# An eight-tap causal convolution on TensorE: another order of its head, dummy matmuls before the first product, and one mid weight summed by DMA

## The chip, the cores and the metric

The kernel runs on one core of a Trainium2 chip. The metric is device time in microseconds (us), as a median over several executions. A trace covers one execution and gives a span that is, in the runs of this case, 1.74 to 2.2 us shorter than the time reported for the same execution.

Engines are named as in the profile: PE is TensorE, DVE is VectorE, ACT is ScalarE, POOL is GpSimd, SP is SyncE. PEld is PE's weight load.

## The reference

```python
# x: (8, 4096, 512) float32, kernel: (8, 512, 512) float32
out = np.zeros_like(x)
for k in range(8):
    shifted = x if k == 0 else np.concatenate(
        [np.zeros((B, k, D), np.float32), x[:, :-k, :]], axis=1)
    out += np.matmul(shifted, kernel[k])
```

Every output row is a sum of eight rows of x, each multiplied by its own 512x512 matrix ("tap").

## The kernel before

The kernel cuts the 32,768 rows into 128 runs of 256 consecutive rows. One run lies on each SBUF partition, and a step handles eight rows of every run, so there are 32 steps. Each step needs x transposed. In steady state an SP DMA does that (`transpose_x`). The first rows are transposed by PE itself: its 16 transposes at 24.51 us took 1.07 us, where a transposed load takes 6.1 us (median).

It saves products by working with sums of x rows (`D4`, `D42`, `D421` and so on, made by DVE) and differences of weights (the "mid" weights, `W[MID, ...]`). A "product" is four matmuls of 128x128 by 128x512: one row of every run by one 512x512 matrix. A step has three "nodes", each for four rows and four taps. A node makes nine products instead of 16 (36 matmuls) and combines them in PSUM through "seeds": copies that ACT writes into a PSUM bank, onto which PE then accumulates. The very first node is computed directly, with 16 products.

The parts that the change and the argument touch:

```python
    def load_x(i, h):                                  # POOL, 512 KB into SBUF
        xin[i, h] = xpool.tile([P, 4, D], bf, name="xin")
        load(xin[i, h], xr[:, K * i + 4 * h:K * i + 4 * h + 4, :])

    def transpose_x(i, h):                             # SP, SBUF to SBUF, transposing
        nc.sync.dma_start_transpose(out=XT[:, 4*h:4*h+4, :]..., in_=xin[i, h]...)

    def mid_dve(*which):                               # DVE, 128x2048 subtraction
        o, u, v = mid(*which)
        tt(o, u, v, SUB)

    def fill(pw):                                      # a pair of dummy matmuls
        for h in range(2):
            nc.tensor.matmul(pw[:, h], lhsT=zero[:, 0:P], rhs=zero, start=True, stop=True)

    def node_seed(n, b_):                              # ACT writes the seed into PSUM
        n.p[b_] = pair((2 * n.k + b_) % 3)
        if b_ == LO: nc.scalar.copy(out=n.p[b_][:, 1], in_=n.q[:, 1])
        else:        nc.scalar.mul(out=n.p[b_][:, 1], in_=n.q[:, 1], mul=-1.0)
    # ... cut ...
    # the head, in program order (cut to what matters)
    transpose_pe("h0", 3, H, 4, 6)                     # rows before the run (history)
    transpose_pe("h1", 0, H, 6, 8)
    nc.scalar.copy(out=to(XF[:, 0:2]), in_=prev(bank["h0"]))
    transpose_pe("x0", 2, xin[0, 0], 0, 2)             # first x rows
    nc.scalar.copy(out=XF[:, 4:6], in_=bank["x0"])
    tt(D4[:, 0:2], XF[:, 0:2], XF[:, 4:6], ADD)
    transpose_pe("xb", 3, xin[0, 0], 2, 4)
    direct(0, 0)                                       # first product: first tap
    # ... cut: nine more products, DVE sums and mid weights ...
    transpose_pe("x1", 2, xin[0, 1], 0, 4)
    # ... cut ...
    transpose_pe("x2", 2, xin[1, 0], 0, 4)             # second step's first x rows, all four
    tt(T4, XT[:, 4:8], XT[:, 0:4], ADD)
    direct(3, 0); fill(pair(2)); direct(3, 1)
    node_a1(1)                                         # needs a DVE sum, then an ACT copy
    # ... cut ...
    mid_dve(0, HI, LO)                                 # the mid weight that the change moves
    # ... cut; then the loop over nodes, the same in both kernels:
    for k, (i, a) in enumerate(order):
        if a == MID and more: transpose_x(i + 1, 0)
        # ... products, seeds, sums ...
        if a == LO and more:
            transpose_x(i + 1, 1)
            load_x(i + 2, 0); load_x(i + 2, 1)
```

## Time and profile before

| | before |
|---|---|
| time, median of 3 | 780.17 us (780.01 to 780.49) |
| traced span | 778.4 us |
| transposed loads (SP), median | 6.1 us from issue to landing, 61 of them |

How busy each engine is, as a whole and stage by stage, and where PE stops is read in the prediction below. Two views that matter later were not used for the prediction. One is the list of DMA queues, from which this line comes; it gives packets, megabytes and the share of the 16 DMA engines.

```profile
q8 instruction: 28, 0.46, 0.2%
```

The reader is to see 28 transfers of about 16 KB each in a queue of their own. 0.2% looks like nothing.

The other is the timeline well inside the steady part. Here are DVE and ACT of the kernel before, around 103 us (start, busy time, engine, line, operation, count; in brackets the idle time before and who ended it):

```profile
102.78 1.23 DVE L76 TENSOR_TENSOR D<-XT 128x2048 bf16<-128x2048 bf16 x1 [0.37 <-DMA XT<-xin]
103.93 1.22 DVE L76 TENSOR_TENSOR y<-pp,ms 128x1024 f32<-128x1024 f32 x1
...
105.98 0.57 ACT L249 COPY pp<-pp 128x512 f32<-128x512 f32 x1 [0.71 <-PE pp L190]
```

DVE waits 0.37 us for a transposed load, then makes the sum D4 and, behind it, the output y, done at 105.15. ACT's seed at 105.98 waits for PE, not for y. With the 0.08 us that a handover from y to the seed takes (seen in the trace after: y done 106.02, seed 106.10), this load could land 0.75 us later before PE felt it.

### The profile page before, as it was taken

The page shows a single profiled execution, that of the slowest core. Times are in us where ns is not written, and L with a number is a line of the kernel's source. Part 1 is how long each engine was busy: PE and PEld are TensorE (multiplying, and loading weights), DVE is VectorE, ACT ScalarE, POOL GpSimd, SP SyncE. Part 2 cuts the span into 40 slices and gives each one's busy share as a digit, 9 for nine tenths or more (in the row PEclk, how much of TensorE's full clock was granted, in tenths as well). Part 3 has the DMA queues.
Part 4 walks back from the last instruction along what each step waited for, and adds up shares of the span by engine and source line. Part 5 has one row for each costly group of instructions (what it writes and reads, how often), then busy time and mean ns, then how long its engine had stood idle before and what let it go on. Part 6 is the DMA issues. An engine that isn't in the chain of part 4 may idle for free.

```text
span 778.4 us, 9432 instructions
## 1 busy us (share of the span) xinstructions
PE 765.6 (98%) x3576; PEld 346.9 (45%) x3576; DVE 658.7 (85%) x767; ACT 282.7 (36%) x461; POOL 41.2 (5%) x79
## 2 busy tenths in 40 slices
PE   6999999999999999999999999999999999999997
PEld 3444444444444444444444444444444444444443
DVE  4999988898888898888898888898888898878895
ACT  3453343333343333343333343333343333343332
POOL 4000000000000000000000000000000000000000
PEclk9999999999999999999999999999999999999999
DMA  9975887877787878787787687877797867687843
GB/s 198 211 125 137 214 198 181 194 166 185 166 177 194 195 166 177 171 194 179 175 189 183 166 202 170 195 168 185 166 192 176 204 162 185 167 181 184 205 132 122
DMA packets 159229, 138.90 MB, mean 178 GB/s; under 512 B 130128, under 2 KB 134224, under 8 KB 159056
## 3 DMA queue, kind: packets, MB, share of 16 engines
q1 hardware_dynamic: 145456, 99.89, 46.0%
q0 software_dynamic: 13584, 38.15, 31.1%
q8 instruction: 28, 0.46, 0.2%
q10 hardware_dynamic: 144, 0.26, 0.1%
q14 instruction: 17, 0.14, 0.1%
HBM read 77.33 MB, written 67.11 MB: 186 GB/s over the span
## 4 chain that ended last, share of the span: by engine, by line
PE 92%; DVE 4%; DMA 2%; issue 1%; POOL 1%; DVEq 0%; ACT 0%; ACTq 0%; POOLq 0%
PE pp L190 92%; DMA xin<-in_x_dram 2%; DVE w L76 2%; DVE D L76 1%; POOL w L80 0%; DVE pp L76 0%; DVE pp L265 0%; DVE XT L383 0%; PE pp L179 0%; DVE y L76 0%; DVE A L76 0%; POOL xin L80 0%; DVEq L635 0%; ACT pp L249 0%; POOL XT L80 0%
## 5 line engine op out<-in xcount | busy, mean ns | idle before, releaser
L190 PE MATMUL pp<-w,D 128*128 128x512 bf16 x3280 | 716.8, 379 | 4.2 <-DMA w<-in_kernel_dram 2.6
L190 PEld LDWEIGHTS <-D 128*128 128x128 bf16 x3280 | 320.4, 98 | 392.8 <-issue 3.3
L76 DVE TENSOR_TENSOR D<-D 128x1024 bf16<-128x1024 bf16 (+1 forms) x252 | 228.4, 945 | 1.0 <-ACT D L346 0.9
L76 DVE TENSOR_TENSOR y<-pp,ms 128x1024 f32<-128x1024 f32 (+1 forms) x121 | 146.2, 1211 | 45.4 <-PE pp L190 45.4
L76 DVE TENSOR_TENSOR D<-XT 128x2048 bf16<-128x2048 bf16 (+2 forms) x153 | 142.3, 945 | 11.2 <-DMA XT<-xin 9.2
L237 ACT COPY pp<-pp 128x512 f32<-128x512 f32 x95 | 54.1, 570 | 255.1 <-PE pp L190 255.0
L249 ACT COPY pp<-pp 128x512 f32<-128x512 f32 x95 | 54.2, 570 | 172.2 <-PE pp L190 170.0
L76 DVE TENSOR_TENSOR pp<-dts,pp 128x512 f32<-128x512 f32 x95 | 65.5, 689 | 43.9 <-ACT dts L255 42.6
L292 ACT COPY ms<-pp 128x1024 f32<-128x1024 f32 x60 | 61.0, 1016 | 33.0 <-PE pp L190 33.0
L80 POOL DMA_DIRECT2D xin<-in_x_dram x64 | 34.0, 532 | 687.2 <-DMA XT<-xin 672.6
L265 DVE SCALAR_TENSOR_TENSOR pp<-pp,dts 128x512 f32<-128x512 f32 x95 | 65.8, 693 | 3.3
L255 ACT COPY dts<-pp 128x512 f32<-128x512 f32 x95 | 57.5, 606 | 2.0 <-PE pp L190 2.0
L251 ACT ACTIVATE pp<-pp 128x512 f32<-128x512 f32 x95 | 56.1, 590 | 0.8 <-DVE y L76 0.8
L190 PE MATMUL pp<-w,XT 128*128 128x512 bf16 x120 | 30.8, 379 | 0.0
L76 DVE TENSOR_TENSOR w<-w,w 128x2048 bf16<-128x2048 bf16 x19 | 22.8, 1217 | 0.3 <-DMA w<-in_kernel_dram 0.2
L190 PEld LDWEIGHTS <-XT 128*128 128x128 bf16 x120 | 11.7, 98 | 14.2
L190 PE MATMUL pp<-w,w 128*128 128x512 bf16 x36 | 9.2, 378 | 1.3 <-ACT pp L237 0.7
L190 PE MATMUL pp<-w,F 128*128 128x512 bf16 x36 | 8.9, 379 | 0.0
L391 ACT COPY XT<-pp 128x1024 bf16<-128x1024 bf16 x1 | 1.0, 1012 | 17.5 <-PE pp L179 17.5
L173 PE MATMUL pp<-zero 128*128 128x512 bf16 x16 | 6.1, 539 | 1.2 <-DVE zero L145 1.2
L331 DVE MEMSET D<- 128x64 bf16 x2 | 0.2, 112 | 7.9 <-ACT D L343 7.7
L80 POOL DMA_DIRECT2D w<-in_kernel_dram x8 | 6.0, 755 | 4.1 <-DMA w<-in_kernel_dram 3.0
(53 smaller groups left out, 69.9 us busy)
## 6 DMA issues: line engine op xcount, KB each, us to landing
out_dram<-y SPq DMA_DIRECT2D x123, 512.0 KB, 3.5
xin<-in_x_dram POOLq DMA_DIRECT2D x64, 512.0 KB, 5.8
w<-in_kernel_dram POOLq DMA_DIRECT2D x8, 512.0 KB, 17.5
D<-in_x_dram SPq DMA_DIRECT2D x1, 1024.0 KB, 4.9
out_dram<-ms SPq DMA_DIRECT2D x2, 512.0 KB, 3.2
out_dram<-f SPq DMA_DIRECT2D x2, 512.0 KB, 4.3
XT<-xin SPq DMA_TRANSPOSE x61, 6.1
XT<-in_x_dram POOLq DMA_DIRECT2D x1, 384.0 KB, 10.9
```

The source lines that it names most:

```text
L76: nc.vector.tensor_tensor(out=o, in0=a, in1=b, op=op)
L80: nc.gpsimd.dma_start(out=out, in_=src)
L173: nc.tensor.matmul(pw[:, h], lhsT=zero[:, 0:P], rhs=zero, start=True, stop=True)
L190: nc.tensor.matmul(bank, lhsT=comp[:, c * P:(c + 1) * P], rhs=w[:, c, :], start=start and c == 0, stop=c == DC - 1, skip_group_check=True)
L237: nc.scalar.copy(out=n.q[:, 0], in_=n.q[:, 1])
L249: nc.scalar.copy(out=n.p[b_][:, 1], in_=n.q[:, 1])
L251: nc.scalar.mul(out=n.p[b_][:, 1], in_=n.q[:, 1], mul=-1.0)
L255: nc.scalar.copy(out=n.dts, in_=n.q[:, 0])
L265: nc.vector.scalar_tensor_tensor(out=p[:, 0], in0=p[:, 1], scalar=-1.0, in1=n.dts, op0=MUL, op1=SUB)
L292: nc.scalar.copy(out=ms[b_], in_=p)
L331: nc.vector.memset(z[:, :, 0:D:G], 0.0)
L391: nc.scalar.copy(out=XT[:, 0:2], in_=bank["x2"][:, 0:2])
```

## The change

Its intent is to bring PE's steady stream forward by three means.

1. Three more pairs of dummy matmuls before the first product, to keep PE busy while it waits; the order of copies and transposes is changed with them. In the trace of before, PE's granted clock was 0.50 from 11.48 to 14.89 us, behind a stretch of 3.42 us with PE busy 1.16; that more work in the waiting time would keep it at 1.00 was the estimate from that.
2. The second step's first four x rows are loaded, transposed and summed two by two, so that the first node can start before all four are there.
3. The mid weight `W[MID, HI, LO]` is no longer a DVE subtraction. ACT writes the negated weight, and a GpSimd-issued DMA adds the other weight to it.

The remaining lines of the diff reorder the first seven nodes around this. The loop is untouched.

```diff
+    def mid_neg(u, v):
+        nc.scalar.mul(out=W[MID, u, v], in_=W[LO, u, v], mul=-1.0)
+    def mid_acc(u, v):
+        nc.gpsimd.dma_start(out=W[MID, u, v], in_=W[HI, u, v], accum_op=ADD)
 ... cut ...
+    fill(pair(2))
     transpose_pe("h0", 3, H, 4, 6)
+    nc.scalar.copy(out=to(XF[:, 0:2]), in_=prev(bank["h0"]))
+    fill(pair(2))
     transpose_pe("h1", 0, H, 6, 8)
-    transpose_pe("x0", 2, xin[0, 0], 0, 2)
+    transpose_pe("x0", 1, xin[0, 0], 0, 2)
 ... cut ...
-    transpose_pe("xb", 3, xin[0, 0], 2, 4)
+    transpose_pe("xb", 0, xin[0, 0], 2, 4)
+    fill(pair(2))
     direct(0, 0)
 ... cut ...
-    load_x(1, 0)
+    load_x(1, 0, 0, 2)
+    load_x(1, 0, 2, 4)
+    mid_neg(HI, LO)
 ... cut ...
-    transpose_pe("x2", 2, xin[1, 0], 0, 4)
+    transpose_pe("x2", 3, xin[1, 0], 0, 2)
+    transpose_pe("x3", 2, xin[1, 0], 2, 4)
+    fill(pair(3))
-    tt(T4, XT[:, 4:8], XT[:, 0:4], ADD)
+    tt(T4[:, 0:2], XT[:, 4:6], XT[:, 0:2], ADD)
+    tt(D41[:, 1], T4[:, 0], T4[:, 1], ADD)
+    node_a1(1)
+    direct(3, 0)
+    tt(T4[:, 2:4], XT[:, 6:8], XT[:, 2:4], ADD)
+    fill(pair(2))
 ... cut ...
+    mid_acc(HI, LO)
-    mid_dve(0, HI, LO)
```

## The prediction

> **What bounds the kernel now.** I read the page's busy shares first, then the stretches by stage, then TensorE's timeline and the chain that ended last for the first 61 us.
>
> ```profile
> PE 765.6 (98%) x3576; PEld 346.9 (45%) x3576; DVE 658.7 (85%) x767; ACT 282.7 (36%) x461; POOL 41.2 (5%) x79
> ```
>
> TensorE (PE) is busy 98% of the 778.4 us span. That is an average, so I cut the run into stages; in each row come the stretch, its length, the busy us and instruction count of PE, PEld, DVE, ACT and POOL, then the granted TensorE clock.
>
> ```profile
> 4.65:8.06 3.41, 1.98 (x20) 1.08 (x19) 0.00 (x0) 2.41 (x3) 1.87 (x3) 1.00 1.05 199
> 8.06:11.48 3.42, 1.16 (x21) 0.98 (x18) 1.54 (x5) 2.41 (x3) 1.29 (x2) 1.00 1.17 193
> 11.48:14.89 3.41, 3.11 (x12) 1.47 (x13) 2.06 (x2) 0.00 (x0) 1.49 (x2) 0.50 1.11 188
> 14.89:24.51 9.62, 8.46 (x45) 3.83 (x43) 8.75 (x10) 0.00 (x0) 0.74 (x1) 1.00 1.18 210
> 24.51:60.67 36.16, 34.38 (x178) 15.78 (x179) 35.25 (x43) 21.69 (x30) 2.14 (x4) 1.00 0.89 151
> 60.67:773.92 713.25, 713.09 (x3300) 322.56 (x3300) 609.48 (x707) 254.91 (x426) 30.12 (x57) 1.00 0.76 179
> ```
>
> From 60.67 us on PE has 3300 instructions in 713.25 us, 0.216 us each, and its gaps come to 0.16 us. The change leaves the loop and this arithmetic alone. So all that can be won lies before 60.67 us, and the end moves by as much as PE's stream is early at that point. In 24.51 to 60.67 DVE is busy 35.25 of 36.16 us: there the vector engine is nearly full too.
>
> ```profile
> 11.78 1.87 PE L190 MATMUL pp<-w,D 128*128 128x512 bf16 x4 [2.56 <-DMA w<-in_kernel_dram]
> 13.44 1.06 PE L173 MATMUL pp<-zero 128*128 128x512 bf16 x2
> 14.29 1.12 PE L179 MATMUL pp<-ident,XT 128*128 128x128 bf16 x12
> 16.47 4.48 PE L190 MATMUL pp<-w,D 128*128 128x512 bf16 x20 [1.05 <-DVE w L76]
> ...
> 24.51 1.07 PE L179 MATMUL pp<-ident,xin 128*128 128x128 bf16 x16
> ...
> 33.63 1.02 PE L190 MATMUL pp<-w,w 128*128 128x512 bf16 x4 [0.66 <-ACT pp L237]
> ...
> 36.18 2.02 PE L190 MATMUL pp<-w,w 128*128 128x512 bf16 x8 [0.66 <-ACT pp L249]
> ...
> 52.63 6.27 PE L190 MATMUL pp<-w,D 128*128 128x512 bf16 x28 [0.35 <-ACT pp L251]
> ```
>
> Start, busy time, engine, line, tiles, count, and in brackets the idle time and who ended it. The first tap ends a 2.56 us wait at 11.78. Its four matmuls start 0.42 us apart, because the clock is at 0.50 then. The chain that ended last (start, length, what) gives the next gate:
>
> ```profile
> 5.94 18.53 DMA xin<-in_x_dram
> 24.51 1.08 PE pp L179 x16
> 25.61 1.24 DVE XT L383
> ```
>
> The second half of the first x rows is issued at 5.94 and lands at 5.94 + 18.53 = 24.47; its transposes start at 24.51. After that this chain runs through DVE up to 60.67.
>
> [...] the clock changes at 11.48 and 14.89, 3.41 us apart, and the half-speed window follows one in which PE was busy only 1.16 of 3.42 us. One busy 1.98 of 3.41 was followed by full clock[...]. [...] queued loads here land about 2.5 us apart (24.47, then 26.56, 29.10, 31.64)[...]. [...] The before trace has none, so its duration is my largest unknown.
>
> **Part 1, the dummy matmuls and the order up to 24.5 us.** Added ahead of the first tap are three pairs of dummy matmuls. At full speed 6 x 0.216 = 1.3 us, all in waiting time. If they keep the clock up, the four first-tap matmuls and the following dummies and transposes save (1.87 + 1.06 + 1.12) / 2, about 2.0 us of engine time at most. But I expect almost nothing of it at the end. First, the transposes of x rows 2-3 now write the bank that held h1, and wait for ScalarE's third copy. ScalarE: copy of h0 from about 8.4, of x0 from 9.8, of h1 from 10.7, at 1.0 us each, so those transposes move from 8.6 to about 11.7. The window 8.06 to 11.48 then has h1, x0 and one dummy pair, some 1.4 us busy of 3.4[...]. The clock may drop all the same.
>
> Second, what follows is gated twice. DVE: copy of xb 12.4, D2 13.1 (1.4 us), D4 14.4, E4 15.1 to 16.0; the products that reuse E4's bank start at 16.1, against 16.47 before. From there PE has 9 products of 4 matmuls plus one dummy pair: 38 x 0.216 = 8.2 us, giving 24.3. In both kernels the same ten products stand ahead of the x1 transposes, which need the load that lands at 24.47. That load's place in the queue is unchanged. So x1 starts at 24.5 in both (24.7 with a dropped clock): **gain 0, perhaps -0.2**.
>
> **Part 2, x rows two by two, from 24.5 us.** The split halves land about 25.7 and 27.0; PE needs them at 27.1 and 27.6: no wait. Before, from 24.51: 16 transposes (0.90), two products (0.86 each), 16 transposes, three products, one dummy pair (0.43), a product, then the first A1 product at 31.94, a 0.82 us stop for ScalarE's copy, next product at 33.63. After: the same work with one dummy pair more, and A1 brought forward ahead of the last direct product, so that this product and the dummy pair cover the copy: A1 at 31.1, the last direct 31.9 to 32.8, dummies to 33.2, next product 33.2. DVE must have D41 ready for A1: copy 25.6, D4 26.9, D41 28.1, D42 28.7, T4 (half, 0.69 instead of 1.23) 29.9, D41 30.5 to 30.9. It fits by 0.2 us. Gain **0.4 us** (33.63 - 33.2): the stop of 0.82 less the dummy pair of 0.43. The stop for the seed at 36.18 stays, since nothing is put between.
>
> **Part 3, one mid weight by ScalarE and DMA.** DVE loses one 128x2048 subtraction: 1.22 us, 1.14 in steps from start to start. ScalarE gains a scaled copy of 128x2048, estimated 1.9 us from its copy of that size in this trace (1.91), in time it idles (17.5 us of idle before its first copy of x2). One sum of 0.42 us also moves before the x1 copy, and splitting T4 costs 0.15. So DVE is ahead by some 1.4 us at 60 us, and less on the way. PE's losses between 36.2 and 60.7, from start-to-start times: 0.13 at 37.2, 0.22 at 46.06, 0.51 at 52.63, 0.05 and 0.21 later; together 1.1 us. The one at 46.06 waits for a DVE subtraction behind D4, which needs the transposed x landing at 43.74, and will hold PE to 0.2 to 0.4 of lead there. The one at 52.63 waits for a ScalarE seed that the new order makes first: gone. The last two follow from DVE's mid weights, which come 0.6 to 1.4 us sooner: mostly gone.
>
> **Sum.** 0 + lead of 0.2 to 0.4 at 46 + 0.5 + 0.2 = **about 1.0 us** earlier, 0.13% of 780.17: 779.2.
>
> **Rivals.** (a) The DMA add lands late. It is issued behind the load that before started at 44.26 and took 6.7 us beside transposes; so issue near 45.5. [...] I estimate 6 to 9 us, landing at 51.5 to 54.5. DVE wants it at about 54.9 (55.47 before). A landing at 57 would stop DVE, then PE, and make 780 to 782. I give a stop 30%. For it: that load's 6.7 us. Against: the DMA engines are partly idle around 45 and 53. (b) The warm clock is worth its whole 2 us because the x1 load lands sooner: 777.5. Against it, the DMA share is over 1.0 in every stretch from 4.65 to 24.51, with the same loads in the same order; 5%. (c) The new order opens stops, such as A1 waiting for DVE with 0.2 us of margin, or later x loads delaying transposes: 779.5 to 781; 20%. (d) Everything at 24.5 to 60.7 is hidden behind DVE and nothing moves: 780.0; 20%.
>
> **Range and chances.** Runs of before spread 0.5 us. My 80% range is 777.9 to 780.8. Faster by 2% means 764.6; even all stops after 24.51 are under 3 us, so it is out of reach but for an error of mine. Slower by 2% needs 15.6 us, which only a gross stall of the DMA add would make.
>
> **What the profile after will show.** Right: x1 transposes at 24.5 with a longer PE wait before them or a start of 16.1 for the second products; A1 about 31.1 and no 0.82 us stop behind it; PE's steady stream reached about 1.0 us sooner; DVE with one fewer subtraction; the DMA add landed before its reader. Wrong: x1 at 23 or sooner, a DVE wait on the DMA add, or a PE wait for T4 or D41 at 31 us.

The forecast's sum came to about 1.0 us (0 for part 1, a lead of 0.2 to 0.4 at 46 us, 0.5 and 0.2), so 779.2 us. "The before trace has none" means a DMA that adds. The 6 to 9 us for it are the estimate; beside them is the 6.7 us of the load ahead of it.

## The result, and the profile after

The changed kernel took 780.79 us (780.42 to 781.59, 4 runs) against 780.09 us (779.83 to 780.49, 4 runs) for the kernel before on the same chip: 1.001, with a 95% interval of 0.9993 to 1.0027. A ratio here is the mean time of one kernel's fast runs over the mean of the other's in the same rounds, so it is not quite the ratio of the two medians. The prediction was 779.2 us: about 1.0 us to win, and none was won.

Line numbers move by nine from before to after: products are L199 (L190 before), transposes L188 (L179), dummies L182 (L173), the first seed L258 (L249). First the busy shares of the changed kernel:

```profile
PE 767.3 (99%) x3586; PEld 348.1 (45%) x3586; DVE 657.3 (84%) x767; ACT 284.7 (37%) x462; POOL 42.8 (5%) x81
```

PE has ten more matmuls (five dummy pairs net) and DVE 1.4 us less work, as intended. Next the stretches, with the same columns as in the prediction:

```profile
8.32:11.75 3.43, 1.42 (x21) 1.18 (x20) 0.81 (x2) 2.87 (x3) 0.00 (x0) 0.98 1.19 209
11.75:15.17 3.42, 3.42 (x17) 1.63 (x15) 2.67 (x4) 0.00 (x0) 2.33 (x4) 0.52 1.17 186
...
60.67:773.92 713.25, 712.61 (x3299) 322.10 (x3296) 608.69 (x708) 254.53 (x425) 30.24 (x57) 1.00 0.76 179
```

The half-speed window is still there, behind a window with PE busy 1.42 us. (The stretches shown are cut 0.13 us late, hence 0.52 and not 0.50: cut from 11.62 to 15.03 us, the clock is 0.50.) And in the long stretch from 60.67 us on, which had 713.09 us busy before, PE now has 712.61: half a microsecond was lost after the point where the prediction had stopped looking. PE's timeline of the head:

```profile
11.56 0.99 PE L188 MATMUL pp<-ident,xin 128*128 128x128 bf16 x8 [2.01 <-ACT D L358]
12.34 1.06 PE L182 MATMUL pp<-zero 128*128 128x512 bf16 x2
13.33 1.85 PE L199 MATMUL pp<-w,D 128*128 128x512 bf16 x4
...
16.90 1.02 PE L199 MATMUL pp<-w,D 128*128 128x512 bf16 x4 [0.62 <-DVE w L76]
...
25.10 1.06 PE L188 MATMUL pp<-ident,xin 128*128 128x128 bf16 x16
...
31.66 1.04 PE L199 MATMUL pp<-w,D 128*128 128x512 bf16 x4
32.54 1.03 PE L199 MATMUL pp<-w,w 128*128 128x512 bf16 x4
33.40 0.59 PE L182 MATMUL pp<-zero 128*128 128x512 bf16 x2
33.83 1.03 PE L199 MATMUL pp<-w,w 128*128 128x512 bf16 x4
```

The transposes of rows 2 and 3 wait 2.01 us for ACT's third copy, as predicted. The first product starts at 13.33 instead of 11.78, the second group at 16.90 instead of 16.47, and the x1 transposes at 25.10 instead of 24.51. From there the order works: A1 at 31.66 has no 0.82 us stop behind it.

To follow PE through the kernel I use ACT's copy of every node's result to SBUF (`dts`), 95 of them, which exist in both kernels. The change moves the copies of nodes 2, 3, 5 and 6 to other places in ACT's order, so these say nothing of PE; the others do. The table gives how much later than before each stands (negative: earlier), at five of them:

| copy of node | before | after |
|---|---|---|
| 1 | 36.04 us | +0.20 |
| 4 | 58.07 us | -0.38 |
| 8 | 91.46 us | -0.56 |
| 10 | 106.95 us | **+0.12** |
| 95 | 768.03 us | -0.13 |

So PE did reach its steady stream earlier, by 0.56 us, and lost 0.68 us again in one place near 106 us. This is that place in the changed kernel's timeline (DVE, ACT, PE):

```profile
103.66 1.23 DVE L76 TENSOR_TENSOR D<-XT 128x2048 bf16<-128x2048 bf16 x1 [2.17 <-DMA XT<-xin]
104.80 1.22 DVE L76 TENSOR_TENSOR y<-pp,ms 128x1024 f32<-128x1024 f32 x1
...
106.10 0.57 ACT L258 COPY pp<-pp 128x512 f32<-128x512 f32 x1 [1.39 <-DVE y L76]
...
106.72 2.53 PE L199 MATMUL pp<-w,D 128*128 128x512 bf16 x11 [0.47 <-ACT pp L258]
```

Read it from the bottom. PE waits for ACT's seed, the seed for DVE's y, and y stands behind the sum D4, which waited 2.17 us (0.37 before) for a transposed load. In the chain that ended last (start, length, what) the same load shows:

```profile
96.31 0.33 SPq L284
...
96.73 6.83 DMA XT<-xin
```

It was issued at 96.73, 0.93 us earlier than before (97.66), and landed at 103.56, 0.87 us later than before (102.69): 6.83 us instead of 5.03. Why the same 512 KB load took 1.8 us longer is what the experiments had to find out.

### The profile page after: what moved, and what is told of

It is laid out like the page before. It is cut to its first block, busy times and chain, and to the rows that moved or that the text cites. A ratio compares the mean times of both kernels' runs of the same rounds, so it can differ in the third digit from the quotient of the medians.

```text
span 778.3 us, 9453 instructions
## 1 busy us (share of the span) xinstructions
PE 767.3 (99%) x3586; PEld 348.1 (45%) x3586; DVE 657.3 (84%) x767; ACT 284.7 (37%) x462; POOL 42.8 (5%) x81
## 4 chain that ended last, share of the span: by engine, by line
PE 95%; DMA 2%; DVE 1%; ACT 1%; issue 0%; DVEq 0%; SPq 0%; ACTq 0%
PE pp L199 94%; DMA XT<-xin 2%; PE pp L188 1%; DMA D<-in_x_dram 1%; DVE D L76 0%; DVE y L76 0%; PE pp L182 0%; ACT pp L258 0%; ACT XT L346 0%; ACT D L357 0%; DVE w L76 0%; ACT XT L349 0%; ACT D L358 0%; DVE pp L76 0%; DVEq L653 0%
## 5 line engine op out<-in xcount | busy, mean ns | idle before, releaser
L199 PE MATMUL pp<-w,D 128*128 128x512 bf16 x3280 | 716.7, 379 | 1.1 <-DVE w L76 0.6
L199 PEld LDWEIGHTS <-D 128*128 128x128 bf16 x3280 | 320.6, 98 | 390.4 <-issue 4.5
L258 ACT COPY pp<-pp 128x512 f32<-128x512 f32 x95 | 54.2, 571 | 171.9 <-PE pp L199 163.2
L199 PE MATMUL pp<-w,XT 128*128 128x512 bf16 x120 | 30.8, 379 | 0.0
L199 PEld LDWEIGHTS <-XT 128*128 128x128 bf16 x120 | 11.7, 98 | 14.2
L182 PE MATMUL pp<-zero 128*128 128x512 bf16 x26 | 9.0, 480 | 1.2 <-DVE zero L147 1.2
L199 PE MATMUL pp<-w,w 128*128 128x512 bf16 x36 | 9.2, 379 | 0.7 <-ACT pp L258 0.7
L199 PE MATMUL pp<-w,F 128*128 128x512 bf16 x36 | 8.8, 379 | 0.0
L188 PE MATMUL pp<-ident,xin 128*128 128x128 bf16 x48 | 3.7, 233 | 2.0 <-ACT D L358 2.0
```

Source lines behind the costliest of these rows:

```text
L188: nc.tensor.transpose(o[:, t - t0, c * P:(c + 1) * P], src[:, t, c * P:(c + 1) * P], ident)
L199: nc.tensor.matmul(bank, lhsT=comp[:, c * P:(c + 1) * P], rhs=w[:, c, :], start=start and c == 0, stop=c == DC - 1, skip_group_check=True)
```

## The experiments

"Lead" below is the position of the `dts` copies against the first trace of before, as in the table above. A second trace of the kernel before (run before_again) has it at +0.02 (+0.04 at the end), so the lead repeats well.

Two theories of the lost microsecond, A and B, stood at the start; C was added after the first four runs below (up to e3).

- **A**: the DMA add is the cause. It delays the loads and transposes around it, and that delay reaches PE at 106 us.
- **B**: the lead is given back at a fixed place, because something there keeps its own time whatever PE does.
- **C**: the load at 97 us is lengthened by another transfer that falls into it, and which of them falls where depends on how many instructions PE has had. Its rival, in the expectations from p1 on, is **D**: the stop comes from the new order of loads and stores, and that transfer is a bystander.

C came from comparing the two DMA views of just this load. First before, from its issue to its landing (queues, then issues with us to landing):

```profile
q1 hardware_dynamic: 2286, 1.30, 100.2%
...
XT<-xin SPq DMA_TRANSPOSE x1, 5.0
```

The same view of the changed kernel, here with its line of GB/s in 40 slices of the window:

```profile
GB/s 0 0 334 382 405 382 334 143 262 286 453 122 172 228 227 213 218 218 215 221 218 219 213 213 216 321 380 395 477 405 405 358 382 72 0 24 0 24 24 24
...
q8 instruction: 1, 0.02, 0.8%
...
XT<-xin SPq DMA_TRANSPOSE x1, 6.8
```

One 16 KB packet of the queue "instruction" lies in the window, and the load ends in a tail of 24 GB/s. The plateau is near 390 GB/s and the profile counts 16 DMA engines, so by my estimate (390 / 16) 24 is what one engine moves; I read the tail as fifteen engines that had finished and one that was late. In the kernel before, PE has 7164 instruction records (matmuls, weight loads and 12 of its sequencer), and 28 packets are there: 7164 / 28 = 256 to a packet, on average; at 0.216 us for a matmul and its weight load, 128 x 0.216 = 27.6 us. That the packets go with the count of PE's instructions is an estimate from these two numbers, which p1 and p2 below put to the test. In the kernel before the packet of this round was at 103.8 us, just after the load had landed. The changed kernel has 20 more PE instructions and is 0.56 us early, and its packet is at 101.5 us.

### after_again: the changed kernel once more

No edit.

> The changed kernel once more, for the spread of its times and a second profile. If the stop of TensorE near 106 us is systematic, the second profile has it again (0.5 to 0.8 us, behind a transposed x that lands at 103 to 104 us); if it was chance, it is missing and TensorE ends 0.6 us sooner, near 772.8. Time 780.4 to 781.3 either way.

Measured: 780.65 us (779.69 to 781.88, 5 runs), before 780.43 (779.82 to 781.18, 9 runs); 1.0004 (0.9992 to 1.0017). This time the clock did not drop in the head: the four matmuls of the first product took 1.02 us (1.85 in the first trace) and stand at 12.91, the second group at 15.91, the x1 transposes at 24.39. The lead is -0.50 at node 1, -0.95 at node 8, -0.61 at node 9, and +0.36 at node 10: again a stop at 106, of 0.97 us. The 0.34 us given back between nodes 8 and 9 came with a wait of DVE for the transposed load before this one (1.35 us, landing at 90.3). So the half-speed window of the first trace was chance: other executions of the same kernel do without it. That holds for the kernel before as well. Its second trace (before_again) has no half-speed window there (mean granted clock of the span 1.000, against 0.996 in the first trace); its first product comes at 11.55, and its x1 transposes, after a wait of 1.39 us for their load, at 24.53, against 24.51 with the clock dropped. The loss that part 1 was to remove is thus not there in every execution, and in the kernel before it cost nothing at x1. The clock doesn't explain the lost time either, because here there was more lead and none of it was left.

### e1_mid_on_dve: the mid weight back on DVE, no DMA add

```diff
-    mid_neg(HI, LO)
-    mid_acc(HI, LO)
+    mid_dve(0, HI, LO)      # behind prep_d42(HI) of node 3's preparation
```

> Undoes one part: the mid weight is again a VectorE subtraction; no ScalarE negation, no DMA add. Theory A (the DMA add delays the next transpose, 56.8 instead of 52.6 us, and through it the x loads, and so makes the stop at 106 us): the transpose lands near 52.7, the stop at 106 us is gone, the lead at 60 us falls from 0.56 to about -0.3 for the 1.14 us more on VectorE, end 0 to 0.3 us later than before, so 780.1 to 780.6. Theory B (the loop hands back any lead at the transposed x near 103 us, add or no add): lead at 60 us the same -0.3, nothing to hand back, time 780.3 to 780.7. If the DMA add costs time outside the traced span, the time less the span falls from 2.1 to 1.8 us.

Measured: 782.22 us (780.79 to 783.58, 5 runs), before 780.43; 1.0023 (1.001 to 1.0035). PE's timeline:

```profile
55.74 3.63 PE L199 MATMUL pp<-w,D 128*128 128x512 bf16 x16 [0.72 <-DVE pp L274]
...
108.22 0.38 PE L199 MATMUL pp<-w,D 128*128 128x512 bf16 x1 [0.92 <-ACT pp L258]
```

That is 1.5 us or more above what either theory expected. Two things follow from the trace. The first is the worth of part 3: with the subtraction on DVE, PE waits 0.72 us for DVE at 55.74, and its lead at node 8 is +0.49 instead of -0.95. Of that 1.4 us, 0.3 were there already at node 1; about 1.1 us is what the DMA add and its order save in the new schedule, as far as one trace of each can say. The second is that the stop at 106 us is there all the same (1.13 us) with no DMA add in the kernel, and that it is as long although PE is now late and not early. A falls, and so does B, under which a kernel 0.49 us late should have lost nothing.

### e2_other_bank: rows 2 and 3 transposed into another bank

```diff
-    transpose_pe("xb", 0, xin[0, 0], 2, 4)
+    transpose_pe("xb", 3, xin[0, 0], 2, 4)
```

> The transposes of x rows 2 and 3 write PSUM pair 3 instead of pair 0, as before the change, so that neither they wait for ScalarE's third copy nor the first-tap products for VectorE's read. Expected in the head: those transposes at 9.4 us, first-tap products at 11.4 us at full clock [...], x1 transposes right behind the landing at 24.2 us, 0.8 us sooner than in the changed kernel. Theory B (a lead is handed back near 103 us): the lead at 60 us grows to about 1.3 us, the stop at 106 us grows by the same, time unchanged within 0.2 us of the changed kernel. Rival (a lead in the head reaches the end): 0.8 us faster than the changed kernel, near 780.0.

This takes those transposes out from behind ACT's third copy, and it undoes a second wait that the prediction had overlooked: the first product goes to bank pair 0, which in the changed kernel still holds those transposes until DVE has copied them (12.58 to 13.27 us in the first trace after). What is left for the first product is the wait for the third copy itself, because h1 lies in pair 0 too. Measured: 781.46 us (780.44 to 781.64, 5 runs); 1.0008 (0.9995 to 1.0022). PE's timeline in the head:

```profile
11.53 1.02 PE L199 MATMUL pp<-w,D 128*128 128x512 bf16 x4 [1.34 <-ACT D L358]
...
24.43 1.07 PE L188 MATMUL pp<-ident,xin 128*128 128x128 bf16 x16 [0.64 <-DMA xin<-in_x_dram]
```

The first product comes at 11.53, 1.4 us before that of after_again (12.91, behind a wait for DVE's copy). The clock was up in both (the four matmuls of the first product took 1.02 us in each), so this is the bank conflict alone. The x1 transposes come at 24.43 against 24.39, now after a wait for their load. So the prediction's step that x1 starts when its load lands holds here, and the conflict costs nothing there when the clock stays up. The kernel was nevertheless not faster: PE stopped for 1.27 us at 46.97 (a packet of the instruction queue at 42.9 us lay inside a transposed load, which took 6.0 us instead of 4.4), so that its lead went from -0.46 at node 1 to +0.33 at node 4, and it lost another 1.06 us at 106.

### e3_no_dummies: the three pairs of dummies before the first product taken out

```diff
-    fill(pair(2))           # before h0, before h1, behind xb
```

> The changed kernel without the three pairs of dummy matmuls ahead of the first tap. The clock drops at 11.5 to 11.8 us with or without them, so theory: first-tap products at 13.3 us at half clock as in the changed kernel, x1 transposes at 25.1 us, time the same within 0.2 us. Rival (they do warm): the clock stays at half for longer, x1 at 25.6 us or later and the time 0.5 us or more longer.

Measured: 781.18 us (780.44 to 782.22, 5 runs); 1.0011 (0.9999 to 1.0024). I expected no change, and the trace shows one: the clock was at half speed twice (7.5 to 10.9 and 14.3 to 17.7 us; 16 transposes took 1.89 us at 7.65, and 1.06 us at 25.80), and x1 started at 25.80, against 25.10 and 24.39 in the two traces with dummies. Between these traces the dummies make 0.7 to 1.4 us of the head, though the clock's windows differ between executions (half speed from 11.62 to 15.03 us in the first trace after, none in the head of after_again) and there is one trace without dummies; in times of whole runs the difference to after_again is only 1.0007, well inside the scatter. The stop at 106 was there again, 1.10 us.

### p1_after_pad26: the packet moved, nothing else

If C is right, the changed kernel wants only a few more PE instructions before 100 us, which do no work that matters. 26 small dummy matmuls (52 instructions with their weight loads) went into places where PE waits anyway.

```diff
+    def pad(pw, n):
+        for _ in range(n):
+            nc.tensor.matmul(pw[:, 0, 0:P], lhsT=zero[:, 0:P], rhs=zero[:, 0:P], start=True, stop=True)
+    pad(pair(2), 13)        # behind the first fill
+    pad(pair(2), 13)        # before the transposes xb
```

> The changed kernel with 26 small dummy matmuls (128 columns, 52 more TensorE instructions with their weight loads) put into TensorE's idle time at 5.8 to 7.6 and 9.4 to 11.5 us. They do no useful work; they only move the 16 KB transfers on the queue marked instruction[...] 52 x 0.108 = 5.6 us earlier: from 101.5 to about 96 us, out of the transposed x load of 97 to 103 us. Theory C (that transfer inside the transposed load makes it last 6.7 instead of 5.0 us, and so makes the stop near 106 us): the load lasts 5.0 us, no stop at 106 us, the lead of 0.6 to 1.0 us over the kernel before is kept to the end, time 779.3 to 779.9, 0.7 to 1.0 us faster than the changed kernel. Theory D (the stop comes from the new order of loads and stores, the transfer is a bystander): stop as before, time 780.5 to 781.

Measured: 779.74 us (779.33 to 779.92, 5 runs), before 780.54 (779.99 to 780.68, 9 runs); 0.999 (0.9978 to 1.0003). The interval touches 1, but all five runs lie below all nine of before. The packet moved from 101.5 to 94.9 us, and the load issued at 96.2 took 5.02 us. The DMA view of the load and the two engines behind it (DVE, then PE):

```profile
q1 hardware_dynamic: 2287, 1.31, 99.0%
...
XT<-xin SPq DMA_TRANSPOSE x1, 5.0
```

```profile
101.33 1.23 DVE L76 TENSOR_TENSOR D<-XT 128x2048 bf16<-128x2048 bf16 x1
...
98.72 10.52 PE L203 MATMUL pp<-w,D 128*128 128x512 bf16 x47
```

DVE doesn't wait for the load at all and PE runs through 106 us without a stop. The lead is -0.58 at node 8, as in the first trace after (-0.56), still -0.58 at node 10, and -0.81 at the end (the kernel before loses 0.27 us near 231 us, in both of its traces, and this kernel doesn't; why isn't shown). The mean of the runs is 0.76 us below that of before.

### p2_before_pad10: the packet pushed into the load of the kernel before

The opposite test: the kernel before with 10 such matmuls (20 instructions), as many as the change adds.

```diff
+    pad(pair(2), 10)        # before the first transposes
```

> The kernel before with 10 small dummy matmuls (20 more TensorE instructions, as many as the change adds) in idle time at 5.6 to 6.7 us. Theory C: the instruction transfer moves from 103.8 to about 101.6 us, into the transposed load of 97.7 to 102.7 us, which then lasts about 6.7 us; a stop of 0.5 to 1.1 us appears near 106 us, time 780.7 to 781.5. Theory D: nothing happens, 780.1 to 780.5, as the kernel before.

Measured in the trace, in the DMA view of the load and on PE:

```profile
q8 instruction: 1, 0.02, 0.8%
...
XT<-xin SPq DMA_TRANSPOSE x1, 6.8
```

```profile
107.28 1.45 PE L194 MATMUL pp<-w,D 128*128 128x512 bf16 x6 [0.74 <-ACT pp L253]
```

The packet went from 103.8 to 102.1 us, into the load; the load took 6.81 us instead of 5.03, and PE stopped for 0.94 us at 106, a stop that the kernel before doesn't have. This is the effect made on purpose, with no part of the change in the kernel, so D falls. It isn't the lead that does it: in g2 below, another variant of the kernel before, the load is issued at the same time (97.32, here 97.31) with a like lead (-0.36, here -0.27); its packet lies outside and its load takes 5.03 us. The times are a half miss: the traced run took 780.90 us, as expected, but the median was 780.49 (780.21 to 780.90, 5 runs) against 780.54, 0.9999 (0.9986 to 1.0013). The head of this kernel was 0.27 us ahead, which pays for part of it. Why the four runs without a trace were not slower can't be seen; the packet was perhaps not inside the load in all of them.

### before_again: a second trace of the kernel before

No edit.

> The kernel before once more, for a second profile. If the place of the instruction transfer is set by the program, it is at 103 to 104 us again, after a transposed load of 5.0 us, and no stop of TensorE near 106 us. Time 780.0 to 780.9.

Measured in one look: 780.24 us. The packet was at 103.9 us, the load, issued at 97.4, took 5.03 us, and the lead against the first trace is +0.02, at the end +0.04. The kernel before misses the packet by about 1.4 us in both traces.

### p4_pad_fewer_fills: p1 without the two dummy pairs behind the x2 and x3 transposes

```diff
+    pad(pair(2), 15)        # in place of 13, twice
-    fill(pair(3))           # behind x3
-    fill(pair(2))           # before node_u
```

> As the first, with the two dummy pairs at 29.5 and 33.4 us taken out and four small dummies put in at the start, so that the count of TensorE instructions is the same. The second pair lies on the path (0.43 us); at the first TensorE would wait for VectorE anyway. Expected 0.2 to 0.4 us less than the first at 36 us; at the end 0 to 0.4 us less: 779.0 to 779.8. Rival: VectorE paces 37 to 60 us and nothing is left of it by then.

The result was wrong (relative error 0.117), so this is no version to use. Its time, 779.89 us (779.72 to 780.07, 5 runs), isn't below that of p1 either. The packet was at 94.8 us, the load took 5.00 us and there was no stop at 106.

### f3_no_fill_3 and f4_no_fill_2: which of the two pairs the result needs

```diff
-    fill(pair(3))           # f3: the first of the two
-    fill(pair(2))           # f4: the second
```

> The changed kernel without the dummy pair that follows the transposes of the first x half into PSUM pair 3. The fourth kernel of the last set lacked two such pairs and was wrong. Theory: ScalarE writes half of that pair next, and matmuls accumulate on it[...]. Then wrong, with a relative error near 0.1. Rival: the other pair did it, and this one is right. Time not of interest.

> The changed kernel without the dummy pair that follows the transposes of the second x half into PSUM pair 2, where the next sums are seeded by ScalarE. By the same theory wrong as well, so that a split into two banks needs two dummy pairs[...]. Rival: right, and the pair only costs its 0.43 us.

Both gave wrong results (relative errors 0.0887 and 0.0993), so both pairs are needed. Times of two runs each: 781.24 and 780.31 us. Why is not shown. The seeds that ACT writes here go into banks that transposes had used before; that a dummy matmul must come in between was the theory, and the errors of these two runs and of p4 (0.117, without both) are all that bears on it. Before the change all four rows went through one pair of banks, with one dummy pair behind them, and the results of f1, g2 and p2, which leave that as it was, are right. Two by two they go through two. That is the "one dummy pair more" of the prediction; these two runs show that the result needs it, whatever it does to the clock, and that its 0.43 us can't be had back by leaving a pair out.

### f1_before_split: the kernel before, with only the x load cut in two

Comparing times with spans left a second loss. In the kernel before, the reported time is 1.74 to 1.84 us above the span of the same execution (also in p2); in the changed kernel and its variants e1 to e3 and p1 it is 2.0 to 2.2 us. That is some 0.36 us which no view of the trace shows. One more DMA is a candidate.

```diff
-    load_x(1, 0)
+    load_x(1, 0, 0, 2)
+    load_x(1, 0, 2, 4)
```

> The kernel before with one thing of the change: the second step's first x rows loaded in two halves, one after the other at the old place. The time exceeds the traced span by 1.74 to 1.84 us in nine runs of the kernel before, and by 2.0 to 2.2 us in every run of the changed kernel and of its variants, the one without the DMA add too. If the additional load makes that, here it is 2.1 to 2.2 us; if not, 1.8 us. Span 778.2 to 778.9 us.

Measured: 780.36 us (2 runs), before 780.12 (779.91 to 781.02, 9 runs); 1.0002 (0.9984 to 1.002). Time minus span is 1.76 us, as in before: the split isn't it.

### p5_bank_and_pad36: both finds together

```diff
-    transpose_pe("xb", 0, xin[0, 0], 2, 4)
+    transpose_pe("xb", 3, xin[0, 0], 2, 4)
+    pad(pair(2), 18)        # behind the first fill
+    pad(pair(2), 18)        # before the transposes xb
```

> The best of both: the changed kernel with x rows 2 and 3 transposed into pair 3, and 36 small dummy matmuls in idle time, which move the instruction transfers 7.8 to 9 us earlier (second from 47 to about 38.5, fourth from 101.7 to about 93). x1 transposes at 24.3 us whatever the clock does, lead over the kernel before 0.9 to 1.1 us at 58 us, no stop at 106 us; time 779.2 to 779.7. If the fourth transfer delays the x load of 90 to 96 us instead, a stop of up to 0.5 us comes back and the time is 779.7 to 780.2.

Measured: 779.60 us (779.32 to 780.15, 5 runs), before 780.12 (9 runs); 0.9994 (0.998 to 1.0008). Packet at 94.4 us, load 5.02 us, no stop at 106; the lead is -0.89 at node 8 and -1.11 at the end, the largest of all, in a span of 777.3 us. Of p1 and p5 neither is shown to be the better; both medians are below those of the changed kernel (780.79 and 780.65, measured in other calls), and every run of p1 is below every run of the kernel before in its call.

### g2_before_dma_add: the kernel before with part 3 alone

```diff
+    mid_neg(HI, LO)
+    mid_acc(HI, LO)
-    mid_dve(0, HI, LO)
```

> The kernel before with one part of the change alone: the mid weight by ScalarE negation and DMA add, no other line moved. TensorE's instructions are as many as before, so the instruction transfer stays at 103 to 104 us. Theory C: no stop near 106 us. VectorE has 1.14 us less to do from 48 us on; of TensorE's losses only the 0.26 us after 54 us are VectorE's, the 0.51 at 52.6 is ScalarE's order and stays: lead at 58 us 0.2 to 0.3 us, kept to the end, time 779.8 to 780.2. Rival (the DMA add delays the transposed load of 47 us to 57 us and this costs later): a new stop, time 780.5 to 781.5. If the add makes the 0.36 us outside the span, time less span is 2.1 us; else 1.8.

Measured: 780.77 us (779.90 to 781.28, 6 runs), before 780.44 (10 runs); 1.0001 (0.9988 to 1.0014). The add landed at 53.64. The packet was at 103.7 us and the load ended at 102.4, so there was no hit and no stop at 106; the lead is -0.36 at node 10 and -0.64 at node 27. The six runs fall into two groups, 779.90 to 780.44 and 781.11 to 781.28, and the traced one is of the second: PE lost 1.33 us there near 386 and 421 us. Ahead of the first, a load with a packet inside took 7.41 us; ahead of the second, a load with no packet inside (the last one was 1.7 us before it) took 10.07 us, so not every late load is the packet's doing. Time minus span is 2.10 to 2.18 us: the DMA add alone, without the rest of the change, comes with the 0.36 us. But e1, without it, has 2.12. What the 0.36 us is stays open.

### g3_before_new_head: the kernel before with part 1 alone

The head up to the x1 transposes is taken from the changed kernel (with the load cut in two); everything behind it is as before.

```diff
-    ... head of before, up to transpose_pe("x1", ...)
+    ... head of the changed kernel: dummies, xb into bank pair 0, its order
     # no mid_neg, no mid_acc; x2 and node 1 as before
```

> The kernel before with the first part of the change alone: dummies, order and loads up to the x1 transposes; behind them all as before. TensorE instructions 16 more than before, so theory C puts the instruction transfer at about 102 us, inside the transposed load: stop of 0.7 to 1.1 us at 106 us. x1 transposes between 24.4 (clock kept up) and 25.1 us (clock dropped), against 24.5. Time 780.6 to 781.6. If the first part makes the 0.36 us outside the span, time less span is 2.1 us here; if the later part makes it, 1.8 us.

Measured: 782.28 us (781.32 to 782.58, 4 runs), before 780.44; 1.0021 (1.0008 to 1.0035), above the 780.6 to 781.6 that were expected. The new head alone is 0.82 us late at node 1 and not early: the clock was at half speed again (12.61 to 16.02 us; mean granted clock of the span 0.998) and x1 started at 25.34. The packet was at 103.4 us and the load, issued at 98.8 because everything is later, was still under way: 6.66 us, and PE stopped:

```profile
108.65 0.59 PE L192 MATMUL pp<-w,D 128*128 128x512 bf16 x2 [0.84 <-ACT pp L251]
```

Here the packet stays near its place of before (103.8): there are 16 PE instructions more, but PE is 0.8 to 1.0 us late. It is the load that moved into it. It is the coincidence that counts, not which of the two moves.

### The traces together

The margin of 0.75 us, read from the kernel before alone, gives the stop to be expected at 106 in every other kernel: how much later than before DVE's sum D4 starts there, less how much later PE is at node 9, less 0.75 us. The stop measured is the step of the lead from node 9 to node 10.

| kernel | packet at | load | D4 later by | PE later by | expected stop | measured stop |
|---|---|---|---|---|---|---|
| before | 103.8 | 5.03 | 0 | 0 | none | none |
| after | 101.5 | 6.83 | +0.88 | -0.56 | 0.69 | 0.68 |
| after_again | 101.7 | 6.59 | +1.12 | -0.61 | 0.98 | 0.97 |
| e1 | 103.0 | 6.76 | +2.37 | +0.49 | 1.13 | 1.13 |
| e2 | 102.7 | 6.68 | +2.04 | +0.22 | 1.07 | 1.06 |
| e3 | 102.7 | 6.72 | +2.10 | +0.25 | 1.10 | 1.10 |
| p2 | 102.1 | 6.81 | +1.43 | -0.27 | 0.95 | 0.94 |
| g3 | 103.4 | 6.66 | +2.80 | +1.00 | 1.05 | 1.05 |
| p1 | 94.9 | 5.02 | -1.45 | -0.58 | none | none |
| p5 | 94.4 | 5.02 | -1.68 | -0.89 | none | none |
| f1 | 104.1 | 5.02 | +0.14 | -0.01 | none | none |
| g2 | 103.7 | 5.03 | -0.34 | -0.36 | none | none |

In every kernel of the table with the packet inside this load the load took 6.6 to 6.8 us and PE stopped; in every one without, 5.02 or 5.03 us, and it did not. The stop is accounted for to 0.01 us by the late load. The three kernels with wrong results, left out of the table, agree: 6.68 and 6.67 us and a stop in f3 and f4, with the packet inside, 5.00 us and none in p4. From 97 us to the end, in the twelve traces of the table, loads of this kind (`transpose_x(i + 1, 1)`) with no packet inside have medians of 5.02 to 5.05 us and a maximum of 5.8; with one inside, 5.0 to 6.9, once 7.4.

The place of the packets in these hits (51 of 348 loads) holds a surprise. 47 start 4.4 to 5.2 us after the load's issue, and none between 0.8 and 4.4. Nor do they come evenly, though PE does: in the kernel before four of them stand at 103.8, 133.2, 157.6 and 188.4 us. From these places I estimate that the loads hold the packets back too, which no run tested, and "packet at" need not be the time at which one was asked for. In 39 hits the packet took 0.9 to 1.2 us and the load 6.6 us or more; in 8 the packet took 1.3 to 1.6 us and the load 5.0 to 5.1. That the coincidence lengthens the load is shown; how a packet of 0.9 us costs it 1.8 us is not. PE itself doesn't stop at a packet of the kernel before: it runs from 98.66 us over the one at 103.8 without a wait.

Most hits further on cost PE nothing: the load of before at 236.66 us took 6.74 us, DVE waited 1.50 us, and PE didn't stop, because that load had been issued about 0.6 us sooner in relation to DVE's work than the one at 97 us.

## Why the prediction was wrong

**The step that failed** is the first one: "the end moves by as much as PE's stream is early at that point", 60.67 us. It rested on PE's gaps of 0.16 us from there on, in the kernel before. That row is right, but it says only that nothing stops PE at the old timing. It doesn't say how much margin the engines and transfers behind it have, nor that a transfer stays as long when its surroundings shift. At 106 us the margin was 0.75 us. The change moved a transfer of 16 KB that no line of the program names into the load that had this margin, and the 0.56 us of lead became 0.12 us of delay at 107 us. For the traced executions that is shown in both directions, by p1 and p2.

**Bounds up to 60 us**: mostly right. Part 2 gave 0.39 us (33.83 against 33.63, with the x1 transposes 0.59 us later); predicted 0.4. Part 3 and the new order took the lead from +0.20 at 36 us to -0.56 at 60 us, so 0.76 us; the sum had about 0.7. By matmuls, 0.51 us of it came at 52.63, exactly the stop that was to go, and the rest behind it. The wait at 46 us did hold PE back as stated: after_again had 0.51 us of lead at 36 us (35.67 against 36.18) and 0.21 at 46 (45.85 against 46.06). In p1 the stop there was 0.58 us, behind a load that took 5.06 us with a packet inside, against 4.43 in after_again; that risk wasn't in the sum. The lead at 60 us came to 0.56 and, with the clock up, 0.95 us, where the sum had 1.0.

**Part 1** was predicted at 0 to -0.2 us. With the clock up it was about that (24.39 against 24.51). In the first trace it was 0.59 us late, beyond that range. The clock did drop (0.50 from 11.62 to 15.03 us, behind a stretch of 3.42 us with PE busy 1.41), which the text left undecided; but in the kernel before the same drop cost nothing at x1 (24.51, and 24.53 in the trace without it). What is new is that the first product had to wait for the bank that held rows 2 and 3 until DVE had copied them, at 12.91 with the clock up; that wait for a reader of the same bank was overlooked. PE then has no time to spare ahead of x1: in after_again it runs up to 24.39 without a wait for the load, where e2 waits 0.64 us and before_again 1.39. That the two together make the 0.59 us is likely but not shown: no trace has the other bank and a dropped clock. Of e3 I had expected that the dummies are worthless in this order; its one trace says otherwise, as without them the head is worse.

**Rivals.** (a) The DMA add wasn't late: issued 44.84, landed 54.05 (9.2 us for 512 KB, beside a load of 6.5 and a transposed load of 9.5), inside the predicted 51.5 to 54.5, and its reader started at 55.13. The transposed load beside it landed at 56.77 instead of the 52.64 of before, with no stop of PE behind it up to 60 us. (b) was wrong, as before_again and e2 show most plainly: with the clock up x1 waits for its load and starts at 24.53 and 24.43. (c), at 20%, had the right kind of outcome, "later x loads delaying transposes", with the wrong cause, since the load that mattered was issued earlier, not later (96.73 against 97.66). (d) was wrong: things did move.

**The size of the miss.** Predicted was -1.0 us; the means of the runs say +0.77 us in the first measurement and +0.32 us in the second (after_again), and the 95% intervals of both ratios include 1. In traces: a lead of 0.56 or 0.95 us in place of 1.0; then 0.68 us lost at 106, or 1.31 us from 91 us on; and about 0.36 us that lies outside the span. The last is measured but not explained: the split load isn't it (f1), nor the dummies and the new head (g3, 1.78 to 1.82 us), the DMA add alone brings it (g2), and yet it is there in e1 without an add. The first pair of traces closes with it: the changed kernel ends 0.13 us ahead (the kernel before loses 0.27 us near 231 us, the changed one doesn't), less 0.36 us outside the span, which is the +0.21 us between the two traced times (780.42 and 780.21). The stop at 106 is not all that moves the times: the five runs of after_again lie between 779.69 and 781.88 us, two of them as fast as p1, and only one was traced. With the packet moved away (p1) the mean is 0.76 us below the kernel before, near the forecast, though its interval reaches 1.0003. So the forecast held up to 60 us but for part 1, and failed at a transfer that it had not looked at.

## What to carry to other kernels

When the engine that bounds a kernel is brought forward, read the margin of every transfer that it depends on later, not only its gaps: a gap-free stretch can hide a load with 0.75 us to spare. In a list of queues look also at the small ones and ask what falls inside a critical load; here 20 more PE instructions brought a 16 KB packet of the queue "instruction" from 103.8 to 102.1 us and so into such a load, which took 6.81 us instead of 5.03 (p2). Where a schedule is tuned to the last microsecond, a handful of padding instructions tests that in one run. Compare a change of less than 0.2% with the trace of both kernels and with a second trace of the same kernel, because the clock's windows differ between executions: here a half-speed window stands in the head of the first trace of each kernel and not in that of the second.
